# Attention of a hybrid encoder step: score products over all 128 partitions, value products in the array's two column halves, samples by zero-padded full-size products

## The chip, the cores and the metric

The kernel runs on one core of one Trainium2 chip. The metric is device time in microseconds, from the start of the program to its end. The kernel before took 2320.24 us (median of 3 runs, 2312.8 to 2323.56). TensorE (PE in the profile) multiplies; VectorE (DVE), ScalarE (ACT) and GpSimd (POOL) do the rest; SyncE (SP) issues the DMAs. Engines run beside each other, each one works through its own instructions in a fixed order, and semaphores hold an instruction back until what it reads is there or the buffer that it writes is free.

## The reference

One layer of an encoder, for 1024 tokens of a prompt and for 8 samples of 16 tokens each. From the normalised rows one projection makes the inputs of three mixers; their outputs are gated and summed, then follow an output projection, a norm, and a feed-forward block with a short convolution. Only the first mixer is touched here, attention over a sliding window: 8 query heads in two groups of 4, each group with one key head and one value head of 64 features, and one sink logit per head that takes part in the softmax but has no value.

```python
# prompt: every chunk of 64 tokens sees itself and the two chunks before it
s = jnp.einsum('bnqgrd,bnkgd->bngrqk', qc, kb, preferred_element_type=F32) * A_SCALE
s = jnp.where((key_pos >= 0)[None, :, None, None, None, :], s, NEG_BIG)
p = sink_softmax(s, sink[:, :, None, None])
o = jnp.einsum('bngrqk,bnkgd->bnqgrd', p.astype(v.dtype), vb)
# samples: 128 cached rows and the 16 new ones, no mask
kk = jnp.concatenate([k_cache.astype(k.dtype), k], axis=1)
s = jnp.einsum('bqgrd,bkgd->bgrqk', q, kk, preferred_element_type=F32) * A_SCALE
...
def sink_softmax(s, sink):
    m = jnp.maximum(s.max(-1, keepdims=True), sink)
    e = jnp.exp(s - m)
    return e / (e.sum(-1, keepdims=True) + jnp.exp(sink - m))
```

## The kernel before

The large products are a queue of blocks (`Queue`, `block`, L257 and L232): 128 columns of a weight by 384 tokens, 8 steps of depth 128, and three matmuls a step, since weights and inputs are held in two float32r parts each. These matmuls write a PSUM tile `psg`. After every second step `block` calls `tick`, which moves on generators that stand beside the queue (`beside`, L216): a generator yields the number of ticks until its next part. So the order in which the program is written mixes large products and small work; a scheduler then orders each engine's instructions by that and by what it holds ready, and may put large products ahead of a small one that waits. Attention (`attention`, L1414) is such a generator. It runs beside 21 blocks (`Q.run()`, L1419) and what is left of it follows in `drain`; then the PSUM banks are shared out anew (L1422), and the other two mixers begin. PSUM tiles here are `p1` (2 buffers), `ch` (2), `p2`, `ms`.

The prompt is worked through in 8 tiles of 128 tokens. `a_parts` splits queries and keys of a tile. Group 0 lies on partitions 0 to 63, group 1 on 64 to 127. `qs` holds a query's first part on the group's own half and its second part on the other half; `ks` holds the key's first part on both halves, `kl` the key's second part on the own half. `a_scores` makes a head's scores, 128 queries by 256 keys (128 in the first tile), with two matmuls into the same place: `qs` by `ks` over 128 partitions, and the own 64 partitions of `qs` by `kl`. DVE adds the mask and takes the maximum (L519, into `sm`, 3 buffers for two groups a tile). `a_out` takes the exponentials on ACT (L535, 8 a tile, with their sums), the sinks and the reciprocals; transposes the unnormalised probabilities on PE (16 a tile, 8 in the first; into `ch`, copied to `pT` by DVE and ACT in turn); multiplies `pT` as stationary operand by 64 columns of the values (2 x 8 matmuls a tile, float32, which PE makes in two passes); then multiplies by the reciprocals on DVE (L567), transposes the result with 4 more transposes, and stores it.

`a_samples` goes through the 8 samples one by one. The cached keys and values are loaded into `sm` buffers, the keys transposed to `kw`. Per sample there are four score products of 64 by 64 tiles of the array, an exponential over 144 keys, two transposes, four products with values (over 128 cached rows and over 16 new ones), a copy, one more transpose and a copy.

Of the kernel before, what the change touches and what calls it, by code (L numbers as in the profile page):

```python
# [45 lines left out]
def shape_constants():  # L46
# [17 lines left out]
    # s in the first half of a pair of blocks of b, t in its second half; columns for the second halves alone  # L64
# [7 lines left out]
def tile_encoder_step(ctx: ExitStack, tc: tile.TileContext, cst, x_prompt, x_sample, cache_k, cache_v, st_hgrn,  # L72
# [18 lines left out]
    # the banks of PSUM, shared out anew for each phase  # L91
# [77 lines left out]
    # per-feature vectors, features on partitions  # L169
# [29 lines left out]
    def prep(pieces, kt=KD, cols=P):  # L199
        """pieces: (part of the raw tile, DRAM view [p, k, c]); the exact two-part split of the weights"""  # L200
# [12 lines left out]
    # work that runs beside the large products: generators, moved on between their parts  # L213
# [18 lines left out]
    def block(hl, xh, xl, n, evict, kt=KD):  # L232
        """features on partitions: [128 columns of the weights, 384 tokens]"""
# [11 lines left out]
    def row_block(lh, ll, rhs, evict):  # L245
        """tokens on partitions: [128 tokens, 512 columns of the weights]"""
# [10 lines left out]
    class Queue:  # L257
        """Blocks of the large products in order; the weights of the next unit are made ahead."""
# [40 lines left out]
    def rsqrt(pool, x, n):  # L299
        """x ** -0.5 on [P, n]: an integer seed and three Newton steps"""  # L300
# [13 lines left out]
    def ln_group(pool, tiles, eps):  # L314
        """tiles: for each, its two halves of 512 features, tokens on partitions -> means and 1 / deviation"""
# [22 lines left out]
    def to_features(pool, xns, n, gname, bname, hi, lo):  # L338
        """normalised rows of three tiles -> scaled, features on partitions, in two parts"""
# [12 lines left out]
    # -mean / deviation and 1 / deviation of each input row: the residual is made anew from the input  # L352
# [51 lines left out]
    # ======== A: banded attention with sinks ========  # L404
# [28 lines left out]
    # the first two units: the tokens that are ready first  # L433
# [23 lines left out]
    # the norm weights carry the half of silu = x (1 + tanh(x/2)) / 2  # L457
# [27 lines left out]
    def a_parts(j):  # L485
        """queries: their two parts on the two halves of the partitions; keys: the first part on both halves, and
        the second; so a product of 128 rows and one of 64 make a score"""
# [3 lines left out]
        qs, ks, kl = small("qs", [P, 2, 4, P], 1, F32R), small("ks", [P, 2, 2 * P], 1, F32R), small("kl", [P, 2 * P], 1, F32R)  # L491
        for g, (a, b) in enumerate(((first, second), (second, first))):
# [3 lines left out]
            V.tensor_sub(kl[a, :w], k, ks[a, g, :w].bitcast(F32))  # L496
# [4 lines left out]
    def a_scores(j, parts):  # L501
# [6 lines left out]
        for g in range(2):  # L508
            gs = slice(64 * g, 64 * g + 64)
# [15 lines left out]
    def a_out(j, sc):  # L525
        kts, w, mx, sms = sc
# [13 lines left out]
        V.reciprocal(sums, sums)  # L540
        yield 2
        po = psum("ms")

        def products(g, i2, pT):
            for ii in range(2):
                i = 2 * i2 + ii
                for kt in range(nk):
                    mm(po[:, (2 * i + g) * 64:(2 * i + g + 1) * 64], pT[:, ii * nk + kt, :],
                       vT[:, kts[kt], 64 * g:64 * g + 64], start=(kt == 0), stop=(kt == nk - 1))

        last = None
        for g in range(2):
            for i2 in range(2):
                ps = psum("ch")
                for ii in range(2):
                    for kt in range(nk):
                        o = (ii * nk + kt) * P
                        tr(ps[:, o:o + P], sms[g][:, 2 * i2 + ii, kt * P:(kt + 1) * P])
                pT = small("pT", [P, 4, P], 2)
                (S.copy if i2 else V.tensor_copy)(pT[:, :2 * nk, :], u3(ps[:, :2 * nk * P]))  # L560
                if last is not None:
                    products(*last)
                last = (g, i2, pT)
                yield 1
        products(*last)
# [1274 lines left out]
```

## Time and profile before

| | us |
|---|---|
| median of 3 runs | 2320.24 |
| lowest, highest run | 2312.8, 2323.56 |
| span of the profiled execution, first to last instruction | 2315.3 |
| TensorE busy in that span | 2256.6 |
| attention beside large products, first score to the last large product | 120.5 to 297.9 |
| rest of attention, no large product beside it | 297.9 to 317.5 |

The profile shows one execution. Its span is told; a whole time for that execution, from start to end of the program, is not given apart from it, and the runs lie from 2.5 us under to 8.3 us over the span. The page gives busy time by engine and the chain of waits that ended last. Matmuls are pipelined: a matmul's length in the timeline holds the way through the array, and what one matmul costs in a row of matmuls is the distance from its start to the next one's start. A float32 product appears as two matmuls, one for each pass; float32r products as one.

### The profile page before, as it was taken

Reading aid. Unit: us, or ns where it says so; the run is one execution under the profiler, and the core shown is the slowest. Engines: PE = TensorE matmul, PEld = TensorE weight load, DVE = VectorE, ACT = ScalarE, POOL = GpSimd, SP = SyncE. Lnnn points to the kernel's source line nnn. Section 1 sums busy time; section 2 is a strip of 40 time slices with the busy share of each in tenths; the row PEclk is TensorE's granted clock in tenths of the full one; section 3 lists DMA queues with packets and bytes.
Section 4 is the critical chain, followed back from the end, with each engine's and each line's share of the span. In section 5 each row is a group of like instructions: output and inputs, shape, how many; then the busy total and the mean of one; then the engine's idle time right before and its main releaser. Section 6 shows DMA issues by size and latency. Waiting matters only on the chain.

```text
span 2315.3 us, 35344 instructions
## 1 busy us (share of the span) xinstructions
PE 2256.6 (97%) x13297; PEld 2101.9 (91%) x13297; DVE 1504.4 (65%) x4324; ACT 927.5 (40%) x2106; POOL 102.8 (4%) x74
## 2 busy tenths in 40 slices
PE   6999999999999999999999999999999999999996
PEld 6988989999999999999999978999999999999994
DVE  7256446667675657766777797676566566656669
ACT  4356434434344446354532333453334333432331
POOL 2000000000000000000000054000000000000004
PEclk9999989999999999999999999999999999999998
DMA  4111222222222221222354552321111110111112
GB/s 132 46 55 43 80 74 62 65 80 67 63 82 60 70 63 54 68 66 78 98 151 134 174 165 74 139 65 47 38 29 56 47 47 21 56 52 42 38 47 82
DMA packets 223836, 168.46 MB, mean 73 GB/s; under 512 B 34427, under 2 KB 213409, under 8 KB 223649
## 3 DMA queue, kind: packets, MB, share of 16 engines
q1 hardware_dynamic: 223664, 166.21, 24.0%
q8 instruction: 104, 1.70, 0.3%
q14 instruction: 68, 0.55, 0.1%
HBM read 126.91 MB, written 40.11 MB: 72 GB/s over the span
## 4 chain that ended last, share of the span: by engine, by line
PE 87%; DVE 7%; ACT 3%; DMA 2%; issue 1%; SPq 0%; POOL 0%; DVEq 0%; ACTq 0%
PE psg L107 72%; PE psp L107 6%; PE psch L107 4%; PE psp L147 2%; PE psms L107 2%; PE psch L147 1%; PE psms L147 1%; DVE yac L1787 1%; DVE lnst L321 1%; DMA x<-d_g 1%; ACT L1185 1%; ACT L1181 0%; DVE nwa L308 0%; DVE nwy L310 0%; DVE whl L206 0%
## 5 line engine op out<-in xcount | busy, mean ns | idle before, releaser
L107 PE MATMUL psg<-hh,whl 128*128 128x384 f32 x2976 | 812.6, 346 | 0.0
L107 PE MATMUL psg<-x1h,whl 128*128 128x384 f32 x2112 | 545.0, 336 | 1.2 <-ACT whl L205 1.2
L107 PEld LDWEIGHTS psg<-hh,whl 128*128 128x128 f32 x2976 | 537.7, 189 | 8.7 <-issue 3.6
L107 PE MATMUL psg<-hl,whl 128*128 128x384 f32 x1488 | 511.3, 344 | 1.5 <-POOL hl L347 1.3
L107 PEld LDWEIGHTS psg<-x1h,whl 128*128 128x128 f32 x2112 | 382.8, 188 | 3.2 <-ACT whl L205 1.5
L107 PE MATMUL psg<-x1l,whl 128*128 128x384 f32 x1056 | 355.5, 337 | 0.6 <-POOL x1l L347 0.6
L107 PEld LDWEIGHTS psg<-hl,whl 128*128 128x128 f32 x1488 | 281.5, 189 | 5.1 <-POOL hl L347 1.6
L107 PE MATMUL psg<-late,g 128*128 128x512 f32 x1080 | 251.2, 391 | 0.0
L107 PEld LDWEIGHTS psg<-late,g 128*128 128x128 f32 x1080 | 201.9, 188 | 42.9
L107 PEld LDWEIGHTS psg<-x1l,whl 128*128 128x128 f32 x1056 | 198.9, 188 | 1.7 <-POOL x1l L347 0.9
L206 DVE TENSOR_TENSOR whl<-wraw,whl 128x1024 fp32r<-128x1024 f32 (+1 forms) x122 | 144.2, 1183 | 68.0 <-ACT whl L205 66.9
L1758 DVE TENSOR_TENSOR yac<-yac,psg 128x512 f32<-128x512 f32 x180 | 123.5, 687 | 91.4 <-PE psg L107 88.0
L107 PE MATMUL psg<-o,whl 128*128 128x384 f32 x720 | 140.1, 345 | 3.1 <-DVE x L1464 1.7
L205 ACT CAST whl<-wraw 128x1024 fp32r<-128x1024 f32 (+1 forms) x122 | 121.4, 995 | 48.0 <-PE psg L107 24.7
L107 PEld LDWEIGHTS psg<-o,whl 128*128 128x128 f32 x720 | 125.8, 191 | 6.7 <-issue 2.1
L107 PE MATMUL psg<-wres,mixh 128*128 128x512 f32 x288 | 92.8, 395 | 3.6 <-DVE x L1464 2.7
L1718 DVE SCALAR_TENSOR_TENSOR va<-xp,fvec,va 128x384 f32<-128x384 f32 x132 | 82.0, 622 | 19.8 <-ACT va L1715 18.1
L1718 DVE SCALAR_TENSOR_TENSOR ga<-xp,fvec,ga 128x384 f32<-128x384 f32 x132 | 81.6, 620 | 8.2 <-ACT ga L1715 6.6
L1747 ACT CAST late<-wraw 128x1024 fp32r<-128x1024 f32 x20 | 20.1, 1047 | 162.6 <-PE psg L107 162.6
L1699 ACT COPY xp<-psg 128x384 f32<-128x384 f32 x88 | 42.2, 480 | 107.0 <-PE psg L107 106.8
L1399 ACT ACTIVATE ga<-psg 128x384 f32<-128x384 f32 x72 | 35.3, 491 | 104.0 <-PE psg L107 88.6
L1556 POOL TENSOR_TENSOR rows<-rows,gbin 128x1024 f32<-128x1024 f32 x9 | 27.7, 3078 | 1087.0 <-ACT rows L1555 1087.0
(449 smaller groups left out, 3260.1 us busy)
## 6 DMA issues: line engine op xcount, KB each, us to landing
wraw<-in_w_in_dram SPq DMA_DIRECT2D x58, 512.0 KB
wraw<-in_w_up_dram SPq DMA_DIRECT2D x44, 512.0 KB
d_g<-ga SPq DMA_DIRECT2D x72, 192.0 KB
wraw<-in_w_down_dram SPq DMA_DIRECT2D x22, 512.0 KB
acc<-d_g SPq DMA_DIRECT2D x48, 192.0 KB
d_o<-sq SPq DMA_DIRECT2D x24, 192.0 KB
xp<-d_o SPq DMA_DIRECT2D x24, 192.0 KB
x<-d_g SPq DMA_DIRECT2D x24, 192.0 KB
```

Source lines behind the costliest of these rows:

```text
L107: PE.matmul(out, lhsT, rhs, start=start, stop=stop)
L147: PE.transpose(out, in_, ident[:n, :n])
L205: S.copy(hl[:, 0, :kt, :cols], raw[:, :kt, :cols])
L206: V.tensor_sub(hl[:, 1, :kt, :cols], raw[:, :kt, :cols], hl[:, 0, :kt, :cols].bitcast(F32))
L321: V.bn_stats(out=st[:, i, :], in_=s_)
L1185: S.activation(s_, hd.f[n], AF.Exp, scale=-1.0)
L1399: S.activation(g, ps, AF.Tanh, scale=0.5)
L1556: G.tensor_mul(t, t, gb[:, 0])
L1699: S.copy(xp[:, 2:2 + NW], ps)
L1718: V.scalar_tensor_tensor(acc[:, :w], xp[:, j:j + w], fvec[:, j, ct:ct + 1], acc[:, :w], ALU.mult, ALU.add)
L1758: lambda ps: V.tensor_add(yac[j][:, cs], yac[j][:, cs], ps))
L1787: V.tensor_mul(y[:, sl], y[:, sl], gg)
```

## The change

Three parts, all in attention.

In `a_parts` the key's second part `kl` gets the shape of `ks`, [128, 2, 256], and is written to both halves (one subtraction more for each group). In `a_scores` the second matmul of a score then takes all 128 partitions of `qs` and `kl`, as the first does.

In `a_out` the probabilities are multiplied by the reciprocals before they are transposed, group 0 on DVE and group 1 on GpSimd. The loop over 128-key tiles is now outside: for each, the four heads of a group are transposed into one PSUM tile, and one product per group has 64 columns of the values as stationary operand, the four heads' probabilities as 512 moving columns, and its result on that group's 64 output partitions. The result is laid out as it is stored, so that the last four transposes and the multiplication on DVE go.

In `a_samples` the samples go two by two. A query tile `qz`, zero but for each group's own features and columns, makes all heads' scores of a sample in one product with `kw`, which now holds the new keys beside the cached ones. Probabilities stand in a zeroed tile `pn`, so that the 16 new rows can be multiplied with the values of all samples; products have the full 128 by 128 size.

```diff
@@ a_parts, a_scores
-        qs, ks, kl = small("qs", [P, 2, 4, P], 1, F32R), small("ks", [P, 2, 2 * P], 1, F32R), small("kl", [P, 2 * P], 1, F32R)
+        qs, ks, kl = small("qs", [P, 2, 4, P], 1, F32R), small("ks", [P, 2, 2 * P], 1, F32R), small("kl", [P, 2, 2 * P], 1, F32R)
...
-            V.tensor_sub(kl[a, :w], k, ks[a, g, :w].bitcast(F32))
+            for half in (a, b):
+                V.tensor_sub(kl[half, g, :w], k, ks[a, g, :w].bitcast(F32))
...
-                    mm(o, qs[gs, g, 2 * i2 + ii], kl[gs, :w], start=False, stop=True)
+                    mm(o, qs[:, g, 2 * i2 + ii], kl[:, g, :w], start=False, stop=True)
@@ a_out
+        for g in range(2):
+            sm = sms[g][:, :, :w]
+            (G if g else V).tensor_mul(sm, sm, bc(sums[:, 4 * g:4 * g + 4], 4, w))
         yield 2
         po = psum("ms")
 
-        def products(g, i2, pT):
...
-                    mm(po[:, (2 * i + g) * 64:(2 * i + g + 1) * 64], pT[:, ii * nk + kt, :],
-                       vT[:, kts[kt], 64 * g:64 * g + 64], start=(kt == 0), stop=(kt == nk - 1))
+        def products(kt, pTs):
+            for g in range(2):
+                mm(po[64 * g:64 * g + 64, :], vT[:, kts[kt], 64 * g:64 * g + 64], pTs[g],
+                   start=(kt == 0), stop=(kt == nk - 1))
...
-        for g in range(2):
-            for i2 in range(2):
+        for kt in range(nk):
+            pTs = []
+            for g in range(2):
                 ps = psum("ch")
...
+                for i in range(4):
+                    tr(ps[:, i * P:(i + 1) * P], sms[g][:, i, kt * P:(kt + 1) * P])
+                pTs.append(small("pT", [P, 4 * P], 3))
+                (S.copy if g else V.tensor_copy)(pTs[g], ps)
...
-        oa = small("oa", [P, 4, 2, 64])
-        V.tensor_mul(oa, po.rearrange("p (i g d) -> p i g d", i=4, g=2),
-                     sums.rearrange("p (g i o) -> p i g o", g=2, o=1).to_broadcast([P, 4, 2, 64]))
         yield 1
-        ps = psum("p2")
-        for i in range(4):
-            tr(ps[:, i * P:(i + 1) * P], oa[:, i].rearrange("p g d -> p (g d)"))
         of = small("oaf", [P, 4, P])
-        S.copy(of, u3(ps))
+        S.copy(of, u3(po))
@@ a_samples
+        kc, vw, qz = big(), big(), big()
...
+        G.memset(qz, 0.0)
+        for g in range(2):
+            gs = slice(64 * g, 64 * g + 64)
+            for i in range(4):
+                G.tensor_copy(qz[gs, :, 64 * g + TB * i:64 * g + TB * (i + 1)], bt(qf[i][gs, TPR:]))
+        kw = small("kw", [P, NB, KS])
+        G.tensor_copy(kw[:, :, P:], bt(kf[:, TPR:]))
...
+        def probabilities(r):
+            ps = psum("p1")[:, :2 * KS].rearrange("p (e k) -> p e k", e=2)
+            for e in range(2):
+                mm(ps[:, e], qz[:, 2 * r + e], kw[:, 2 * r + e])
...
+                V.tensor_scalar_mul(o[:, :P], pe[:, e, :P], sm2[:, e:e + 1])
+                V.tensor_scalar_mul(o[:, c:c + TB], pe[:, e, P:], sm2[:, e:e + 1])
...
+            for e in range(2):
+                for c in range(2):
+                    mm(po[:, e * P:(e + 1) * P], (vT[:, 8, :] if c else vw[:, 2 * r + e, :]),
+                       pT[:, (2 * e + c) * P:(2 * e + c + 1) * P], start=(c == 0), stop=(c == 1))
```

How the order changes is shown at three places. Names are those of the tiles, with a number for each use.

First, PE in the middle of the prompt's tiles. `psp` takes scores, `psms` products with values, `psch` transposed probabilities, `psg` large products. Before:

```order
L107 MATMUL psp_212_1471<-ks_1328,qs_1327 128x256
L107 MATMUL psp_212_1471<-kl_1329,qs_1327 128x256
L107 MATMUL psp_212_1471<-ks_1328,qs_1327 128x256
L107 MATMUL psp_212_1471<-kl_1329,qs_1327 128x256
L107 MATMUL psms_1524<-vT,pT_1530 128x64 x4
L147 MATMUL psch_1561<-call,sm_1312 128x128 x4
L107 MATMUL psms_1524<-vT,pT_1549 128x64 x4
L147 MATMUL psch_1578<-call,sm_1312 128x128 x4
L107 MATMUL psg_1747<-hl_2_129,whl_1217 128x384
```

After, products with values (`psms`) and the scores beside them:

```order
L107 MATMUL psp_268_1764<-ks_1609,qs_1608 128x256
L107 MATMUL psp_268_1764<-kl_1610,qs_1608 128x256
L107 MATMUL psp_268_1764<-ks_1609,qs_1608 128x256
L107 MATMUL psp_268_1764<-kl_1610,qs_1608 128x256
L107 MATMUL psms_1671<-pT_1703,vT 64x512
L107 MATMUL psms_1671<-pT_1731,vT 64x512
L107 MATMUL psg_2323<-hh_2_105,whl_1860 128x384
```

In place of four matmuls of 64 columns a head pair there stand two products of 512 columns next to each other, one for each group, and the score products have the same form throughout.

Second, PE where the large products beside attention run out. Before (`kw`, `kf` and `oa` are the samples' keys and queries, `obs` and `pTs` belong to the samples too):

```order
L107 MATMUL psg_3039<-hl_2_150,whl_2722 128x384
L107 MATMUL psg_3039<-hh_2_126,whl_2722 128x384
L107 MATMUL psp_517_3083<-kw_2673,oa_2689 64x128
L107 MATMUL psp_517_3083<-kf,oa_2689 64x16
L107 MATMUL psp_517_3083<-kw_2673,oa_2689 64x128
L107 MATMUL psp_517_3083<-kf,oa_2689 64x16
L147 MATMUL psp_459_2776<-call,obs_2755 128x64
L107 MATMUL psms_2841<-sm_2674,pTs_2819 64x64
L107 MATMUL psms_2841<-sm_2663,pTs_2819 64x64
L107 MATMUL psms_2841<-sm_2674,pTs_2819 64x64
L107 MATMUL psms_2841<-sm_2663,pTs_2819 64x64
```

After (`sm_2084` and `sm_2099` are the seventh tile's probabilities, `sm_2531` the cached keys, `sm_2250` the eighth tile's probabilities):

```order
L107 MATMUL psg_2911<-hl_2_150,whl_2630 128x384
L107 MATMUL psg_2911<-hh_2_126,whl_2630 128x384
L147 MATMUL psch_2357<-call,sm_2084 128x128 x4
L107 MATMUL psms_2330<-pT_2336,vT 64x512
L107 MATMUL psms_2330<-pT_2349,vT 64x512
L147 MATMUL psch_2389<-call,sm_2099 128x128 x4
L107 MATMUL psms_2330<-pT_2362,vT 64x512
L107 MATMUL psms_2330<-pT_2394,vT 64x512
L147 MATMUL psp_419_2547<-call,sm_2531 128x128 x4
L147 MATMUL psp_420_2553<-call,sm_2531 128x128 x4
L147 MATMUL psms_2476<-call,l_386_2377 27x128
L147 MATMUL psch_2455<-call,sm_2250 128x128 x4
```

Before, the last large product stands behind the score products of five samples, and the next one comes behind the last sample. After, it stands inside the seventh tile: the second half of that tile, the whole output of the eighth and all samples stand behind it without a large product between them, and the samples' cached keys are transposed ahead of the eighth tile's probabilities.

Third, ACT at the same place: `kw` takes the cached keys' transposes, rows with `pT` copy transposed probabilities. Before:

```order
L205 CAST whl_2722<-wraw_2720 128x1024
L574 COPY oaf_2534<-psp_412_2529 128x512
L603 COPY kw_2673<-psp_439_2677 128x512
L603 COPY kw_2673<-psp_440_2683 128x512
L560 COPY pT_2631<-psch_2626 128x512
L824 COPY xp_2763<-psg_2725 128x384
L838 ACTIVATE acc_2768<-xp_2763,vec 128x384
L842 ACTIVATE xp_2763<-acc_2768 128x384
```

After (rows with `sums` are the eighth tile's exponentials):

```order
L562 COPY pT_2394<-psch_2389 128x512
L843 COPY xp_2832<-psg_2799 128x256
L844 COPY xp_2832<-psg_2799 128x8x16
L571 COPY oaf_2416<-psms_2330 128x512
L606 COPY kw_2545<-psp_419_2547 128x4x128
L606 COPY kw_2545<-psp_420_2553 128x4x128
L537 ACTIVATE sm_2250,sums_2419<-sm_2250,anm_2421 128x256 x4
L537 ACTIVATE sm_2265,sums_2419<-sm_2265,anm_2421 128x256 x4
L540 ACTIVATE aes_2432<-aes_2432 128x8
```

The eighth tile's exponentials now stand behind the two copies of the samples' cached keys; before, all of the prompt's exponentials were ahead of these copies.

## Rows read from the trace of the kernel before

**Rows 1.** The page: span, engine PE, chain of waits by engine.
```profile
span 2315.3 us, 35344 instructions
...
PE 2256.6 (97%) x13297; PEld 2101.9 (91%) x13297; DVE 1504.4 (65%) x4324; ACT 927.5 (40%) x2106; POOL 102.8 (4%) x74
...
PE 87%; DVE 7%; ACT 3%; DMA 2%; issue 1%; SPq 0%; POOL 0%; DVEq 0%; ACTq 0%
```

**Rows 2.** Stretches of attention: busy us (instructions) by engine, granted clock, DMA share, GB/s.
```profile
120.50:297.90 177.40, 177.40 (x1087) 157.53 (x1087) 94.15 (x317) 92.81 (x265) 1.00 (x4) 0.99 0.20 59
297.90:317.50 19.60, 17.26 (x101) 10.94 (x101) 9.01 (x40) 8.63 (x35) 0.00 (x0) 0.61 0.13 40
317.50:322.80 5.30, 5.30 (x19) 5.20 (x19) 0.06 (x1) 1.32 (x7) 0.00 (x0) 0.50 0.42 118
```

**Rows 3.** Timeline of PE: start us, length us, line, op, out<-in, shapes, count.
```profile
148.40 0.33 PE L107 MATMUL psg<-hl,whl 128*128 128x384 f32 x1
148.58 0.34 PE L107 MATMUL psg<-hh,whl 128*128 128x384 f32 x1
148.75 1.00 PE L107 MATMUL psms<-vT,pT 128*128 128x64 f32 x8
149.56 0.36 PE L107 MATMUL psp<-ks,qs 128*128 128x256 f32 x1
149.85 0.38 PE L107 MATMUL psp<-kl,qs 64*128 64x256 f32 x1
150.17 0.38 PE L107 MATMUL psp<-ks,qs 128*128 128x256 f32 x1
```

**Rows 4.** PE groups by form, 120.5 to 317.5: count, busy us, mean ns, idle.
```profile
L107 PE MATMUL psp<-kl,qs 64*128 64x256 f32 x56 | 21.3, 381 | 0.0
L107 PE MATMUL psp<-ks,qs 128*128 128x256 f32 x56 | 20.1, 358 | 0.0
...
L107 PE MATMUL psms<-vT,pT 128*128 128x64 f32 x240 | 29.3, 271 | 0.0
...
L147 PE MATMUL psch<-call,sm 128*128 128x128 f32 x120 | 18.6, 285 | 0.0
...
L147 PE MATMUL psp<-call,oa 128*128 128x128 f32 x32 | 4.9, 276 | 0.0
```

**Rows 5.** Timeline of PE: a float32 product of 512 columns, two passes.
```profile
504.23 1.02 PE L107 MATMUL psch<-wx,kT 128*128 128x512 f32 x2
```

**Rows 6.** Timeline of PE around products that fill part of the array's columns.
```profile
893.02 0.26 PE L107 MATMUL psp<-mt 128*32 128x32 f32 x4
...
897.19 0.45 PE L107 MATMUL psp<-mt 128*64 128x64 f32 x4
897.57 0.49 PE L107 MATMUL psch<-r,u 128*128 128x128 f32 x2
```

**Rows 7.** Groups by form on ACT, DVE and POOL.
```profile
L535 ACT ACTIVATE sm<-sm,anm 128x256 f32<-128x256 f32 x56 | 27.7, 496 | 3.2 <-DVE anm L532 3.0
...
L519 DVE CUSTOM_DVE_ANT_0 sm<-psp,early 128x256 f32<-128x256 f32 x56 | 21.2, 421 | 16.9 <-PE psp L107 16.9
...
L206 DVE TENSOR_TENSOR whl<-wraw,whl 128x1024 fp32r<-128x1024 f32 x8 | 9.8, 1222 | 9.6 <-ACT whl L205 9.6
...
L603 ACT COPY kw<-psp 128x512 f32<-128x512 f32 x2 | 1.1, 591 | 1.4 <-PE psp L147 1.4
...
L606 POOL COPY oa<-qf 128x128 f32<-128x128 f32 x4 | 1.0, 296 | 223.2 <-PE psp L147 223.2
...
L1556 POOL TENSOR_TENSOR rows<-rows,gbin 128x1024 f32<-128x1024 f32 x9 | 27.7, 3078 | 1087.0 <-ACT rows L1555 1087.0
```

**Rows 8.** Timeline: the load of the samples' cached keys, and their transposes.
```profile
259.12 0.38 SPq L110 DMA_DIRECT2D sm<-in_cache_swa_k_dram  x1
...
264.21 0.27 PE L147 MATMUL psp<-call,sm 128*128 128x128 f32 x1
```

**Rows 9.** Timeline of POOL: the longest multiply of 128x1024.
```profile
1353.17 6.52 POOL L1556 TENSOR_TENSOR rows<-rows,gbin 128x1024 f32<-128x1024 f32 x1 [4.06 <-ACT rows L1555]
```

More of the change, by code (lines that the diff above doesn't have):

```diff
@@ L508, in a_scores @@
         for g in range(2):
-            gs = slice(64 * g, 64 * g + 64)
             sm = small("sm", [P, 4, 2 * P], 3)
@@ L590, in a_samples @@
     def a_samples():
-        vnew = small("sm", [P, 4, 2 * P], 3).rearrange("p a (b k) -> p (a b) k", b=2)[:TB]
-        for b in range(NB):
-            load(vnew[:, b, :], vT[16 * b:16 * b + 16, 8, :])
-        kc = small("sm", [P, 4, 2 * P], 3).rearrange("p a (b k) -> p (a b) k", b=2)
-        kw = small("kw", [P, NB, P])
-        vw = small("sm", [P, 4, 2 * P], 3).rearrange("p a (b k) -> p (a b) k", b=2)
+        KS = P + TB
+        big = lambda: small("sm", [P, 4, 2 * P], 3).rearrange("p a (b k) -> p (a b) k", b=2)
+        kc, vw, qz = big(), big(), big()
         load(kc, cache_k[0].rearrange("b t g d -> t b (g d)"))
         load(vw, cache_v[0].rearrange("b t g d -> t b (g d)"))
+        G.memset(qz, 0.0)
[5 more added lines that the diff above has]
+        G.tensor_copy(kw[:, :, P:], bt(kf[:, TPR:]))
         for i in range(2):
@@ L602, in a_samples @@
                 tr(ps[:, b * P:(b + 1) * P], kc[:, 4 * i + b, :])
-            S.copy(kw[:, 4 * i:4 * i + 4, :], u3(ps))
-        qg = small("oa", [P, NB, 4, TB])
-        for i in range(4):
-            G.tensor_copy(qg[:, :, i, :], bt(qf[i][:, TPR:]))
+            S.copy(kw[:, 4 * i:4 * i + 4, :P], u3(ps))
+        pn = small("sm", [P, 4, 2 * P], 3)
+        G.memset(pn, 0.0)
         oss = small("oaf", [P, 4, NB, TB])
-        for b in range(NB):
-            t0 = TPR + TB * b
-            ps = psum("p1")
+        def probabilities(r):
+            ps = psum("p1")[:, :2 * KS].rearrange("p (e k) -> p e k", e=2)
+            for e in range(2):
+                mm(ps[:, e], qz[:, 2 * r + e], kw[:, 2 * r + e])
+            mx = small("mxs", [P, 6], 3)
+            V.reduce_max(mx[:, 0:2], ps, axis=AX.X)
+            V.scalar_tensor_tensor(mx[:, 2:4], mx[:, 0:2], A_SCALE, sinkc.to_broadcast([P, 2]), ALU.mult, ALU.max)
+            V.tensor_scalar_mul(mx[:, 4:6], mx[:, 2:4], -1.0)
+            yield 1
+            pe = small("pes", [P, 2, KS], 1)
+            sm2 = small("sm2", [P, 4], 3)
+            for e in range(2):
+                S.activation(pe[:, e], ps[:, e], AF.Exp, bias=mx[:, 4 + e:5 + e], scale=A_SCALE, accum_out=sm2[:, e:e + 1])
+            V.tensor_sub(sm2[:, 2:4], sinkc.to_broadcast([P, 2]), mx[:, 2:4])
+            S.activation(sm2[:, 2:4], sm2[:, 2:4], AF.Exp)
+            V.tensor_add(sm2[:, 0:2], sm2[:, 0:2], sm2[:, 2:4])
+            V.reciprocal(sm2[:, 0:2], sm2[:, 0:2])
+            for e in range(2):
+                o, c = pn[:, 2 * (r % 2) + e], P + TB * (2 * r + e)
+                if r > 1:
+                    V.memset(o[:, c - 4 * TB:c - 3 * TB], 0.0)
+                V.tensor_scalar_mul(o[:, :P], pe[:, e, :P], sm2[:, e:e + 1])
+                V.tensor_scalar_mul(o[:, c:c + TB], pe[:, e, P:], sm2[:, e:e + 1])
@@ new lines, in a_samples @@
+        yield from probabilities(0)
+        for r in range(NB // 2):
+            if r + 1 < NB // 2:
+                yield from probabilities(r + 1)
+            yield 1
+            ps = psum("ch")
+            for e in range(2):
+                for c in range(2):
+                    tr(ps[:, (2 * e + c) * P:(2 * e + c + 1) * P], pn[:, 2 * (r % 2) + e, c * P:(c + 1) * P])
+            pT = small("pT", [P, 4 * P], 3)
+            S.copy(pT, ps)
+            yield 1
+            po = psum("ms")
+            for e in range(2):
+                for c in range(2):
+                    mm(po[:, e * P:(e + 1) * P], (vT[:, 8, :] if c else vw[:, 2 * r + e, :]),
+                       pT[:, (2 * e + c) * P:(2 * e + c + 1) * P], start=(c == 0), stop=(c == 1))
@@ L631, in a_samples @@
-            pT = small("pTs", [P, 2, P])
-            S.copy(pT[:, 0, :], ps2[:, :P])
-            S.copy(pT[:TB, 1, :], ps2[:TB, P:2 * P])
-            yield 1
-            ps3 = psum("ms")
-            for g in range(2):
-                gs = slice(64 * g, 64 * g + 64)
-                mm(ps3[:64, gs], pT[:, 0, gs], vw[:, b, gs], start=True, stop=False)
-                mm(ps3[:64, gs], pT[:TB, 1, gs], vnew[:, b, gs], start=False, stop=True)
-            ob = small("obs", [64, P])
-            V.tensor_copy(ob, ps3[:64, :P])
@@ L642, in a_samples @@
-            yield 1
-            ps4 = psum("p2")
-            tr(ps4[:, :64], ob)
-            S.copy(oss[:, :, b, :], bt(ps4[:, :64]))
+                (V.tensor_copy if g else S.copy)(
+                    oss[gs, :, 2 * r:2 * r + 2, :],
+                    po[gs, :2 * P].rearrange("p (e x) -> p e x", e=2)[:, :, 64 * g:64 * g + 64].rearrange(
+                        "p e (i t) -> p i e t", t=TB))
         store(d_o[0][:, TPR:].rearrange("(i p) t -> p i t", p=P), oss.rearrange("p i b q -> p i (b q)"))
```

30 lines of the change are left out of this document (2 added, 28 removed).

## Prediction

> **What bounds the kernel now.** The page comes first: TensorE is busy for 2256.6 of 2315.3 us, and the chain of waits is TensorE's for 87% [rows 1]. The table of stretches then says whether that holds where the change is made. From 120.5 to 297.9 us TensorE is busy for 177.40 of 177.40 us, VectorE for 94.15 and ScalarE for 92.81; from 297.9 to 317.5, with no large product left, TensorE has gaps and a granted clock of 0.61 [rows 2]. So in the first stretch the distance between starts of matmuls is what counts, and VectorE and ScalarE have some 47% to spare; in the second the chain between engines counts.
>
> The timeline gives the distances [rows 3]. A large matmul of 384 columns takes 0.174 us (148.40 to 148.58 to 148.75). The score products have only 256 columns, yet take 0.29 (149.56 to 149.85) and 0.32 (149.85 to 150.17): here a product in the 128*128 form follows one in the 64*128 form and the other way round. By columns alone 256 would be 0.174 x 256/384 = 0.12. Eight matmuls of the values take 0.81 (148.75 to 149.56), 0.10 each, though 64 columns would be 0.03. The mean lengths by form [rows 4] hold the way through the array and are not used as costs; their counts are.
>
> **The change part by part.** First stretch, before, by start distances: 492 large matmuls x 0.174 = 85.6; 112 wide scores x 0.30 and 16 of the first tile at about 0.25 = 37.6; 240 matmuls of the values x 0.10 = 24.2; 32 transposes of `oa` and 120 of the probabilities at 0.10, as for a matmul of few columns, = 3.2 and 12.0; 8 of the cached keys 0.8. That is 163.4; the other 14.0 of 177.4 are the samples' first part, small transposes and a stretch of lower clock.
>
> After, in the same stretch (until the large products run out):
> - Scores: 112 x 0.12 + 16 x 0.11 = 15.2. The price between is 0.12, if only the change of form cost time, and 0.30, if something else in these products does. I take 0.12, since the large matmuls, all of one form, run at 384/0.174 = 2.2 columns a ns, near one in each cycle of the 2.4 GHz level (granted clock 0.99, [rows 2]).
> - Values: 22 products of 512 columns, in 11 pairs. A float32 product of 512 columns takes 1.02 in two passes [rows 5], of which the way through the array is some 0.16 (0.33 less 0.174, [rows 3]); so 0.43 a pass. The two of a pair fill different column halves. If they run beside each other a pair costs 0.86, with 0.10 to come into the form, 0.10 to leave it and 0.05 for a second weight load: 1.11. If one after the other, 1.96. No row shows two 512-column products in different halves. The nearest are four products of 32 columns in four quarters, begun and ended within 0.26 us [rows 6], which leaves some 0.02 for each beyond the first's way; four one after another at 0.10 would be nearer 0.5. I take 1.11: 12.2.
> - Transposes: 96 of the probabilities x 0.10 = 9.6; those of `oa` are gone.
> - Large matmuls: 85.6 as before. Other: about 1.
>
> The sum is 123.6, which is 53.8 less. But not all of it is gained. Before, five samples' scores and all eight tiles were done when the last large matmul was issued; after, half of the seventh tile, the output of the eighth and all samples stand behind it, as the order of PE shows at its second place.
>
> Tail after, as a chain from the last large matmul:
> - The seventh tile's second half ends at about 2.4, which frees an `sm` buffer for the cached keys. Load to first transpose was 5.1 before (259.12 to 264.21, [rows 8]): 7.5. If the buffer were free earlier this falls away.
> - Eight transposes (0.8) and two copies on ScalarE of 0.59 [rows 7]: with waits 9.2.
> - ScalarE works in order, and its third place shows the eighth tile's eight exponentials behind those copies: 8 x 0.49 [rows 7] = 3.9, so 13.2; sinks and reciprocals 0.6, so 13.8.
> - The multiplication on GpSimd of 128 by 1024 took 3078 ns on average [rows 7] and up to 6.52 [rows 9], in a stage where VectorE and DMAs are at work; those of VectorE's size, 1222 [rows 7]. I take 3.1: 16.9.
> - 16 transposes, four copies and two pairs of products at the lower clock, some 5.2: 22.1.
> - The query tile `qz` needs a buffer, a memset (from 0.1 to 8 x 0.296 = 2.4) and eight copies at 0.296 or under [rows 7]; partly beside the above: 26.9.
> - The first two rounds of the samples, from scores to stored result, some 10 with every wait, and three more rounds at 2.8 each: 45.
>
> Before, that stretch was 19.6 [rows 2], in which the samples' 2.4 us rounds were already running. The 5.3 us at half clock that follow [rows 2] stay in both. So 177.4 + 19.6 = 197.0 becomes 123.6 + 45 = 168.6: 28.4 less. From this I take 1.5 for waits of TensorE in the first stretch: 27.
>
> What hides the rest: VectorE gains 16 subtractions of 0.42 (size as in L519) and 8 multiplications of 1.22 [rows 7], 16.5 us; with the 94.15 it stands at 111 of 124 us at most, before what it loses (the multiplication of `oa`, the samples). ScalarE loses nothing of size and stands at about 93 of 124. Within a tile, the way from a free `sm` buffer to the next is four masks and maxima (4 x 0.42), small steps 0.4, eight exponentials 3.9, sinks and reciprocals 0.7, a multiplication of 1.22 or 3.1: 8 to 10 us. TensorE has some 123.6/8 = 15 us of work a tile, of which about 12.5 lie between, so 2.7 to 4.5 us are spare. If that cover goes, every us over it counts about six times.
>
> After attention the orders differ by small swaps only, so no further term. The forecast is 27 less: on the profiled execution's own span 2315.3 - 27 = 2288, and from the median, which lies 4.9 over that span (the start and end of the program and the spread of the runs), 2320.2 - 27 = **2293 us**.
>
> **The rivals.**
> 1. The column halves run one after the other. Each pair then costs 1.96: 11 x 0.85 = 9.4 and four pairs in the tail 3.4 more, about 13 in all: 2306. For it: the products are long, and no row has two such. Against it: the quarters of [rows 6].
> 2. A middle way: the second half's first pass has to wait for the first half's second pass, since matmuls are issued in order and each product is two passes. A pair costs 0.43 more, 15 pairs 6: 2299. The Trainium skill, "TensorE: Matmul & The Clock Gate", section "The mechanism", says that matmuls start and end strictly in program order with no reordering; by that rule this rival would hold if a first pass shares time only with its neighbour. The rows here show only products too short to tell.
> 3. The tail keeps more than the 0.61 of the clock or its waits overlap better, so that it takes 35: 2283. For it: the chain above adds every wait in turn. Against it: TensorE idles in it even more than before.
> 4. Slower: the GpSimd multiplication decides in each tile. With 3.1 the way through a tile is 1.7 + 0.4 + 3.9 + 0.7 + 3.1 = 9.8 of the 12.5 between, so it is hidden up to 5.8 us; beyond that each of six tiles waits, and the tail takes the excess over 3.1 once. At the 6.52 of [rows 9] that is 6 x 0.7 + 3.4 = 7.6 of the gain: 2301. At 9.3 the gain of 27 is used up (6 x 3.5 + 6.2), and at 11 it is 6 x 5.2 + 7.9 = 39: 2332, slower than before. For it: one multiplication of this size took twice the mean, and beside VectorE's own work. Against it: the mean of nine is 3.08, and none reached 7. The Trainium skill, "GPSIMD Engine Reference", section "Specifications", says that this engine's path to SBUF is shared with VectorE, with contention where a VectorE instruction has two SBUF inputs. No row here takes the two apart; by this rule the long one of [rows 9] is what VectorE's subtractions and multiplications beside it make, which speaks for this rival.
> 5. The change does not do what it says: score products cost 0.30 in one form too. That takes 22 from the gain: 2315, and with the long tail it may be over 2320.
>
> **How the numbers follow.** The forecast has 0.66, with a range of its own of 2282 to 2304 (tail 35 to 50, waits up to 5). Rival 1 has 0.10, rival 2 0.06, rival 3 0.08, rival 4 0.06, of which 0.03 is slower than before by over 0.5%, rival 5 0.04, of which 0.01. The range of 2277 to 2311 takes in all but rival 5, the slow part of rival 4, and the ends of the others. About 0.5% (11.6 us) is what a measurement can tell from no change: faster lies under 2308.6, slower over 2331.8. Faster holds the forecast, rivals 2 and 3, most of 1 and half of 4: 0.87; same has rival 5 and the rest: 0.09; slower 0.04.
>
> **What would show it.** In the profile after: start distances of the score products at 0.12 (right) or near 0.3 (rival 5); two `psms<-pT,vT` products of a pair within about 1.1 (right), 1.5 (rival 2) or 1.9 (rival 1); the time from the last large matmul of attention to the next one at about 45 rather than 19.6, with a granted clock near 0.5; ScalarE's copies of `kw` ahead of the eighth tile's exponentials, with TensorE idle before their transposes; and TensorE's idle time before the `psch` transposes, put down to GpSimd's multiplication (rival 4). The forecast is wrong above all if the tail is much longer than 50 us, or if TensorE waits for more than 2 us in each tile.

## The result and the profile after

The changed kernel takes 2282.09 us (median of 4 runs, 2279.38 to 2285.45), the kernel before in the same comparison 2318.52 (2312.8 to 2323.56): ratio 0.9846, 95% interval 0.9829 to 0.9863. The forecast was 2293, with 2277 to 2311 as its range.

The page of the profiled execution, first the span, then TensorE and the other engines, then the chain of waits by engine, against [rows 1]:

```profile
span 2283.7 us, 34763 instructions
...
PE 2210.5 (97%) x12997; PEld 2061.2 (90%) x12997; DVE 1515.1 (66%) x4331; ACT 924.6 (40%) x2085; POOL 125.2 (5%) x89
...
PE 86%; DVE 7%; ACT 3%; DMA 2%; issue 1%; POOL 0%; SPq 0%; DVEq 0%; ACTq 0%; POOLq 0%
```

The span is 31.6 us shorter, and TensorE is busy for 46.1 less. So TensorE lost work, but a third of that came back as idle time. Where, the table of stretches tells (busy us and instructions of PE, PEld, DVE, ACT, POOL, then granted clock), from the first score to the last large product, from there to the next large product, and 5 us beyond; it answers to [rows 2]:

```profile
120.99:246.48 125.49, 125.49 (x766) 113.48 (x766) 89.94 (x272) 78.56 (x218) 18.09 (x7) 1.00 0.24 69
246.48:286.67 40.19, 23.93 (x117) 15.48 (x116) 21.24 (x86) 19.38 (x61) 6.74 (x11) 0.79 0.20 59
286.67:291.67 5.00, 5.00 (x30) 4.96 (x31) 2.53 (x9) 1.88 (x8) 0.00 (x0) 1.00 0.48 131
```

The first stretch shrank from 177 to 125.5, the second grew from 20 to 40.2, with TensorE idle for 16.3 of it. Together 165.7 in place of 197. (In the experiments both are counted from the first score to the next large product, by which the kernel before has 176.6 + 19.9 = 196.5.) TensorE's timeline around one group of scores and one pair of products of the values, against [rows 3]:

```profile
236.59 0.28 PE L107 MATMUL psp<-ks,qs 128*128 128x256 f32 x1
236.70 0.28 PE L107 MATMUL psp<-kl,qs 128*128 128x256 f32 x1
236.82 0.28 PE L107 MATMUL psp<-ks,qs 128*128 128x256 f32 x1
236.94 0.28 PE L107 MATMUL psp<-kl,qs 128*128 128x256 f32 x1
237.06 0.34 PE L107 MATMUL psg<-hh,whl 128*128 128x384 f32 x1
...
237.59 0.28 PE L107 MATMUL psp<-kl,qs 128*128 128x256 f32 x1
237.80 1.08 PE L107 MATMUL psms<-pT,vT 128*64 128x512 f32 x4
238.81 0.44 PE L107 MATMUL psg<-hl,whl 128*128 128x384 f32 x1
239.09 0.51 PE L107 MATMUL psg<-hh,whl 128*128 128x384 f32 x2
```

Scores now start 0.12 us apart (236.59, 236.70, 236.82, 236.94); before it was 0.30. The row with x4 is a pair of products, two passes each: 1.01 from its start to the next matmul's. The score ahead of it takes 0.21 instead of 0.12, and the large matmul behind it 0.28 (238.81 to 239.09) instead of 0.174, so with the changes of form a pair costs 1.20, where 1.11 was forecast. In the records the four matmuls start at 237.801, 237.807, 238.281 and 238.287: first pass of one half, first pass of the other, then the second passes.

In the second stretch TensorE's long waits are these (the bracket has the idle time before, and what ended it):

```profile
250.92 1.08 PE L107 MATMUL psms<-pT,vT 128*64 128x512 f32 x4 [1.37 <-DVE pT L562]
253.50 1.97 PE L147 MATMUL psp<-call,sm 128*128 128x128 f32 x8 [1.50 <-DMA sm<-in_cache_swa_k_dram]
255.26 0.42 PE L147 MATMUL psms<-call,l 128*27 128x128 f32 x1
262.15 1.09 PE L147 MATMUL psch<-call,sm 128*128 128x128 f32 x4 [6.47 <-DVE sm L545]
263.81 1.97 PE L147 MATMUL psch<-call,sm 128*128 128x128 f32 x8 [0.57 <-POOL sm L545]
...
269.57 1.25 PE L107 MATMUL psp<-kw,sm 128*128 128x144 f32 x8
```

The 6.47 us before the eighth tile's transposes are put down to VectorE's multiplication (L545), but that took 1.22; ScalarE's timeline shows what it stood behind:

```profile
255.51 0.58 ACT L606 COPY kw<-psp 128x512 f32<-128x512 f32 x1 [0.27 <-PE psp L147]
256.17 0.51 ACT L537 ACTIVATE sm<-sm,anm 128x256 f32<-128x256 f32 x1
...
259.63 0.49 ACT L537 ACTIVATE sm<-sm,anm 128x256 f32<-128x256 f32 x1
```

The eight exponentials begin right behind the copies of the cached keys, as the third piece of the order said. These copies are not alone in holding them: `anm`, which the exponentials read, was written only until 256.08. VectorE had it behind a copy that waited for TensorE's transpose at 255.26, and this one stood behind the transposes of the cached keys:

```profile
255.72 0.28 DVE L821 COPY r27c<-psms 27x128 f32<-27x128 f32 x1 [1.94 <-PE psms L147]
255.93 0.15 DVE L534 TENSOR_SCALAR anm<-am 128x8 f32<-128x8 f32 x1
```

### The profile page after: what moved, and what is told of

It is laid out like the page before. It is cut to its first block, busy times and chain, and to the rows that moved or that the text cites. A ratio compares the mean times of both kernels' runs of the same rounds, so it can differ in the third digit from the quotient of the medians.

```text
span 2283.7 us, 34763 instructions
## 1 busy us (share of the span) xinstructions
PE 2210.5 (97%) x12997; PEld 2061.2 (90%) x12997; DVE 1515.1 (66%) x4331; ACT 924.6 (40%) x2085; POOL 125.2 (5%) x89
## 4 chain that ended last, share of the span: by engine, by line
PE 86%; DVE 7%; ACT 3%; DMA 2%; issue 1%; POOL 0%; SPq 0%; DVEq 0%; ACTq 0%; POOLq 0%
PE psg L107 74%; PE psp L107 5%; PE psch L107 4%; PE psp L147 1%; PE psms L147 1%; PE psms L107 1%; PE psch L147 1%; DMA x<-d_g 1%; DVE yac L1799 1%; ACT L1197 1%; DVE lnst L321 0%; ACT L1193 0%; DVE mix L1477 0%; DMA wraw<-in_w_out_dram 0%; DVE mixl L1582 0%
## 5 line engine op out<-in xcount | busy, mean ns | idle before, releaser
L1730 DVE SCALAR_TENSOR_TENSOR va<-xp,fvec,va 128x384 f32<-128x384 f32 x132 | 82.0, 622 | 19.8 <-ACT va L1727 18.1
L1759 ACT CAST late<-wraw 128x1024 fp32r<-128x1024 f32 x20 | 20.1, 1047 | 162.6 <-PE psg L107 162.6
```

Of the source, the lines that this page charges most:

```text
L1730: V.scalar_tensor_tensor(acc[:, :w], xp[:, j:j + w], fvec[:, j, ct:ct + 1], acc[:, :w], ALU.mult, ALU.add)
L1759: S.copy(hl[:, 0], raw)
```

## Experiments

"First" is the stretch beside the large products, "second" from the last of them to the next one, both in us of the profiled execution; times are medians, ratios against the kernel before of the same comparison (its medians differ from one comparison to the next, as the first row shows, so that two kernels of different comparisons are compared by their ratios).

| kernel | first | second | both | time | ratio (95%) |
|---|---|---|---|---|---|
| before | 176.6 | 19.9 | 196.5 | 2314.7 to 2319.3 | 1 |
| changed | 125.5 | 40.2 | 165.7 | 2282.1 | 0.9846 (0.9829 to 0.9863) |
| 1 scores alone | 151.4 | 18.2 | 169.6 | 2294.2 | 0.9900 (0.9869 to 0.9932) |
| 2 values alone | 151.0 | 51.9 | 202.9 | 2325.8 | 1.0041 (1.0025 to 1.0058) |
| 3 samples alone | 176.9 | 6.6 | 183.5 | 2305.5 | 0.9952 (0.9933 to 0.9971) |
| 4 changed, old values | 152.6 | 4.1 | 156.7 | 2279.3 | 0.9844 (0.9816 to 0.9872) |
| 5 one column half | 140.3 | 33.8 | 174.1 | 2291.1 | 0.9894 (0.9863 to 0.9924) |
| 6 all on VectorE | 125.8 | 41.1 | 166.9 | 2283.9 | 0.9853 (0.9833 to 0.9872) |
| 7 four buffers | 140.7 | 16.2 | 157.0 | 2274.4 | 0.9811 (0.9789 to 0.9834) |
| 8 both of 6 and 7 | 137.8 | 18.2 | 156.0 | 2273.4 | 0.9808 (0.9780 to 0.9836) |
| 9 more buffers | 142.0 | 13.2 | 155.3 | 2276.5 | 0.9813 (0.9792 to 0.9835) |
| 10 pairs kept | 136.2 | 12.6 | 148.8 | 2263.4 | 0.9763 (0.9745 to 0.9781) |

**1 to 3: each part alone.** Number 1 has the hunks of `a_parts` and `a_scores`, 2 those of `a_out`, 3 those of `a_samples`, each on the kernel before.

Scores, expected: 

> The kernel before with the change of the scores alone (both products of a score on 128 partitions; the samples' saved key rows stand in another buffer so that the tiles fit). Theory: the alternation of forms was the cost, so 112 score products fall from 0.30 to 0.12 us and 16 from 0.25 to 0.11, 22 us less in the stretch beside the large products (177 to 155), and the part behind it stays near 20: about 2297. Rival: the second part of the key costs time for another reason (its place, its split), the pitch stays near 0.3: 2318.

Values, expected: 

> The kernel before with the change of the values alone (probabilities normalised first, products of 512 columns in column halves; the old samples' queries stand in another buffer so that the tiles fit). Theory: TensorE saves 17.6 us (24.2 + 3.2 + 12.0 of matmuls and transposes become 12.2 + 9.6), but a tile's way gets longer by the multiplication, so the large products run out before the samples begin, as after the whole change; the part behind them grows from 20 to 45 or 50 us: 2315, little or nothing gained. Rival: what TensorE saves is gained: 2301.

Samples, expected: 

> The kernel before with the change of the samples alone. Theory: the four rounds of two samples are short enough to stand beside the large products; the part without large products falls from 20 to about 4, the stretch beside them stays near 177: 2301. Rival: the samples are as late as before and the part behind stays at 15 or more: 2314.

The stretches of 1, of 2 and of 3, in this order (columns as in the result, then DMA share and GB/s):

```profile
120.98:272.39 151.41, 151.41 (x1081) 148.16 (x1081) 99.00 (x334) 92.73 (x268) 1.00 (x4) 1.00 0.24 69
272.39:290.55 18.16, 16.70 (x102) 10.66 (x101) 8.61 (x37) 7.75 (x32) 0.00 (x0) 0.68 0.14 43
```

```profile
121.07:272.05 150.98, 150.98 (x767) 120.76 (x766) 85.09 (x260) 79.17 (x218) 17.25 (x7) 1.00 0.19 58
272.05:323.93 51.88, 38.07 (x206) 22.85 (x205) 23.20 (x98) 22.31 (x81) 3.84 (x5) 0.63 0.16 47
```

```profile
120.91:297.81 176.90, 176.90 (x1076) 159.03 (x1076) 96.47 (x340) 96.32 (x277) 4.92 (x10) 0.99 0.20 58
297.81:304.43 6.62, 3.37 (x19) 2.59 (x18) 2.77 (x7) 2.21 (x5) 0.00 (x0) 0.79 0.38 109
```

In 1 and 3 the theory holds: the scores give 26.9 of attention's 196.5, the samples 13.0 (20.6 and 9.2 in the medians). In 2 it holds in kind, and misses in size: the values alone save 25.6 beside the large products (151.0 for 176.6, part of it samples that moved out) and add 32.0 behind them, and the kernel is 0.4% slower than before, where no loss was expected.

**4: the changed kernel without the part on the values.**

> The changed kernel with the old products of the values (scores and samples changed, the values not). If the change of the values carries its 17.6 us of TensorE into the time, this is slower than the changed kernel by that: 2299. Theory: that saving is given back by the longer way of a tile; without it the samples stand beside the large products, attention takes 155 beside them and about 3 behind: 2278, as fast as the changed kernel or up to 8 us faster.

```profile
120.93:273.56 152.63, 152.63 (x1085) 151.13 (x1085) 102.62 (x357) 96.50 (x278) 3.80 (x10) 1.00 0.23 68
273.56:277.65 4.09, 1.52 (x11) 1.13 (x10) 1.84 (x4) 1.58 (x3) 0.00 (x0) 1.00 0.13 48
```

In the profiled executions attention is 9.0 us shorter without the values' part than with it (156.7 and 165.7), and 39.8 shorter than before, which is what 1 and 3 give together (26.9 + 13.0). The times don't show the 9 us: the ratios are 0.9844 and 0.9846. So the whole gain of the change is that of scores and samples, and the values' part gains nothing here; that it costs something in the whole change is seen in the profiles alone (by itself, in number 2, it costs 0.4% of the time). The values' part shortens the first stretch by 27.1 us and lengthens the second by 36.1.

**5: both groups in one column half.**

```diff
-                mm(po[64 * g:64 * g + 64, :], vT[...], pTs[g], ...)
+                mm((pq if g else po)[:64, :], vT[...], pTs[g], ...)
```

> The changed kernel with the products of both groups on the same 64 output partitions, that is in the same column half of the array, in two PSUM tiles; the copy of the result takes two instructions of half the partitions. Theory: the halves work beside each other only if they are different; a pair of products (four matmuls, 1.01 us from its start to the next matmul's in the changed kernel) takes about 1.9, 11 pairs beside the large products make that stretch 9 us longer (135), the part behind it 2 to 3: 2293. Rival: the passes follow each other anyway and the pair is short for another reason: still 1.0, 2282.

```profile
239.08 1.07 PE L107 MATMUL psms<-pT,vT 128*64 128x512 f32 x2
239.99 1.02 PE L107 MATMUL psp<-pT,vT 128*64 128x512 f32 x2
240.94 0.66 PE L147 MATMUL psch<-call,sm 128*128 128x128 f32 x4
```

Same sizes, same form, next to each other, only the same half: 0.91 + 0.95 = 1.86 for the pair instead of 1.01. (Of the 12 pairs beside the large products 7 are parted by other work in this kernel; they take 2 x 1.00.) The theory of the halves holds. Attention is 8.4 longer, and not 12, and by other terms than expected: the first stretch is 14.8 longer, the second 6.4 shorter, since more of the work now lies beside large products and of the second stretch's idle time 8.8 us are left (33.75 less 24.93 busy) in place of 16.3:

```profile
261.24:294.99 33.75, 24.93 (x106) 15.67 (x105) 16.40 (x61) 16.76 (x54) 6.74 (x11) 0.80 0.22 61
```

**6: GpSimd's multiplication on VectorE.**

```diff
-            (G if g else V).tensor_mul(sm, sm, bc(...))
+            V.tensor_mul(sm, sm, bc(...))
```

> The changed kernel with both groups' probabilities multiplied on VectorE. In the changed kernel GpSimd's 2.84 us end 2.98 after VectorE's multiplication begins, and VectorE's subtractions beside it take 1.25 instead of 0.42. Theory: the two engines keep each other out of the same tile memory; two multiplications on VectorE take 2.44 in a row, and no subtraction is stretched, so each tile's way is 0.5 to 1.5 shorter and attention 4 to 8 us (165.7 to about 160): 2277. Rival: GpSimd's multiplication is hidden, and VectorE gets 8 x 1.22 = 9.8 us more to do: 2282 to 2288.

The theory rested on these rows of the changed kernel, VectorE's and then GpSimd's:

```profile
206.66 1.22 DVE L545 TENSOR_TENSOR sm<-sm,sums 128x1024 f32<-128x1024 f32 x1
207.85 2.50 DVE L497 TENSOR_TENSOR kl<-kf,ks 64x256 fp32r<-64x256 f32 x2
...
211.39 0.85 DVE L497 TENSOR_TENSOR kl<-kf,ks 64x256 fp32r<-64x256 f32 x2
```

```profile
206.80 2.84 POOL L545 TENSOR_TENSOR sm<-sm,sums 128x1024 f32<-128x1024 f32 x1 [19.13 <-DVE sums L542]
224.86 2.84 POOL L545 TENSOR_TENSOR sm<-sm,sums 128x1024 f32<-128x1024 f32 x1 [15.22 <-ACT oaf L571]
239.77 2.84 POOL L545 TENSOR_TENSOR sm<-sm,sums 128x1024 f32<-128x1024 f32 x1 [12.07 <-ACT oaf L571]
```

Two subtractions take 2.50 while GpSimd multiplies (until 209.64) and 0.85 when it doesn't. One by one, only the first is long, 2.07, and ends 0.28 behind GpSimd's multiplication; the second takes its 0.42, so that the 1.25 of the expectation is a mean of two unlike ones. The Trainium skill, "GPSIMD Engine Reference", section "Specifications", has this engine's SBUF interface shared with VectorE, with contention for VectorE instructions with two SBUF inputs; the trace agrees. At one place in number 7 (below) GpSimd's multiplication began first, and there it took 1.89, and VectorE's instruction beside it 2.90 where the same form takes 1.22 [rows 7]:

```profile
176.99 1.89 POOL L545 TENSOR_TENSOR sm<-sm,sums 128x1024 f32<-128x1024 f32 x1 [8.71 <-DVE sums L542]
```

```profile
177.07 2.90 DVE L206 TENSOR_TENSOR whl<-wraw,whl 128x1024 fp32r<-128x1024 f32 x1 [0.25 <-ACT whl L205]
```

So by these rows some 0.95 of the 2.84 (2.84 less 1.89) comes with VectorE's multiplication, which began 0.14 before it. This contention costs nothing all the same: with all of it on VectorE, attention takes 166.9, 1.2 more. My theory that it lengthens attention falls, the rival holds.

**7 and 8: a fourth buffer for probabilities.** GpSimd's rows above also show how slow a tile is: the multiplications start 18 and 15 us apart there, and 15 to 22 over all full tiles, more than the 12.5 of TensorE's work that I had put between. Three buffers for two groups a tile let only one group of the next tile begin before this one is transposed. In the kernel with four, the samples' output stands in a buffer of `qs`:

```diff
-            sm = small("sm", [P, 4, 2 * P], 3)
+            sm = small("sm", [P, 4, 2 * P], 4)
...
-                pTs.append(small("pT", [P, 4 * P], 3))
+                pTs.append(small("pT", [P, 4 * P], 2))
...
-        of = small("oaf", [P, 4, P])
+        of = small("pT", [P, 4 * P], 2).rearrange("p (i t) -> p i t", i=4)
```

> The changed kernel with four buffers for probabilities instead of three; to fit, transposed probabilities have two buffers instead of three and share them with the tile that is stored. Theory: the tile's way is long because the second group of the next tile waits for a buffer; with four the next tile's scores and maxima are done before, the eighth tile is out before the large products end, and only the samples stand behind them: 131 beside and 26 behind, 157 in place of 165.7: 2274. Rival: what limits a tile is the order exponentials, multiplication, transposes, copies itself, or the fewer buffers behind: no gain, 2282 or more.

> Both: four buffers for probabilities, and both multiplications on VectorE. Theory: the gains add, 153 for attention: 2270. Rival, if VectorE or the buffers limit: 2278 or more.

```profile
120.93:261.67 140.74, 140.74 (x815) 118.96 (x815) 103.46 (x309) 87.64 (x247) 22.76 (x18) 1.00 0.24 71
261.67:277.88 16.21, 11.75 (x68) 7.33 (x67) 10.42 (x48) 9.48 (x33) 0.00 (x0) 1.00 0.22 63
```

Number 7 is as the theory has it in sum (157.0 for 157), but that is luck: the second stretch is 16, not 26, and the first 10 longer than expected. The tiles do come faster: from the second tile's first exponential to the seventh's it is 15.5 us a tile, against 18.2 in the changed kernel. It is 13.0 in number 4, which has three buffers too, so that three buffers are slow only together with the values' longer way. Number 8 cannot be told from 7, as number 6 alone gained nothing either. The first stretch should have been near 131, and the order of PE shows why it wasn't. With the copies to `pT` at other times, 8 of 15 pairs of products had other work between their two products; 7 of them lie in the first stretch, and its products take 20.1 us there in place of the 13.1 that 13 whole pairs would.

**9 and 10: pairs parted and pairs kept.** Number 9 has three buffers for `pT` again (two small tiles from ahead of attention share buffers of others to make room) and results of products in two PSUM banks in turn. Number 10 is 9 and this, which pins group 0's product behind group 1's:

```diff
-            for g in range(2):
-                mm(po[64 * g:64 * g + 64, :], ...)
+            for g in (1, 0):
+                ins = PE.matmul(po[64 * g:64 * g + 64, :], ...)
+            tc.keep_in_program_order(ins)
```

> The changed kernel with four buffers for probabilities, three for transposed ones (also used for the tile that is stored), and the results of products taken in turn in two PSUM banks. In the order of PE 6 of the 15 pairs of products have other instructions between their two products (8 of 15 with four buffers before this, none in the changed kernel). Theory: a pair that is parted costs 1.9 in place of 1.0, since each half works alone; so the stretch beside the large products is about 5 longer than with whole pairs: 138, and the part behind, with the samples in two banks, 12 in place of 16: 150 for attention, 2268. Rival: parted pairs cost nothing since large products stand between them: 145.

> The same, and the pairs held together: group 1's product is issued first and group 0's pinned behind it (14 of 15 pairs next to each other). Theory: 5 pairs x 0.9 = 4.5 us less than with parted pairs: 145 to 146 for attention, 2263, the fastest of all. Rival: holding a product back delays others, and the time is as with parted pairs: 2268.

TensorE in number 9, a parted product and a whole pair:

```profile
226.26 1.07 PE L107 MATMUL psp<-pT,vT 128*64 128x512 f32 x2
227.26 0.45 PE L107 MATMUL psg<-hh,whl 128*128 128x384 f32 x1
...
239.47 1.08 PE L107 MATMUL psms<-pT,vT 128*64 128x512 f32 x4
240.48 0.66 PE L147 MATMUL psch<-call,sm 128*128 128x128 f32 x4
```

One product alone takes 1.00 of TensorE's time (226.26 to 227.26), two as neighbours 1.01 (239.47 to 240.48). Number 9 is a miss (2276 for 2268, and 155.3 of attention for 150: it gained nothing on 7). Number 10 is the fastest of all, 6.5 us shorter in attention than 9, of which the five pairs that are no longer parted make 5:

```profile
120.89:257.12 136.23, 135.95 (x823) 118.67 (x823) 104.40 (x311) 89.09 (x254) 22.55 (x18) 1.00 0.25 76
257.12:269.70 12.58, 8.55 (x60) 6.97 (x60) 8.77 (x45) 7.70 (x25) 0.00 (x0) 1.00 0.20 58
```

That its median is the 2263 expected is partly luck: attention took 148.8 and not 145 to 146, and of the 14.5 us between the spans of the profiled executions of 9 and 10 (2276.1 and 2261.6) 8 lie behind attention, between some 1000 and 1460 us, where both do the same work. With the eighth tile's output beside large products, only the samples' last rounds are left behind them, and the values' part is worth something now: 148.8 against the 156.7 of number 4, with ratios of 0.9763 and 0.9844 whose intervals don't overlap. Number 4 was not run with four buffers; with TensorE busy for all of its first stretch, and only 4.1 us in the second, there is little for them to gain, but that is argued and not shown.

## Why the prediction was right, and where it was not

**The size.** 27 us were forecast, and 2293 us. Attention gave 31 (197 to 165.7), the spans differ by 31.6, and the medians by 36.4. The 4.8 between spans and medians are the spread of executions: the changed kernel's profiled one took 2285.45, 3.4 over its median and 1.75 over its span; if that 1.75 holds for the kernel before as well, its profiled one took 2317.1, 1.5 under its median. The 4.9 that I set between span and median was thus mostly spread. So of the 9 us that the medians gave beyond the forecast about half are attention's, and the rest lies in that spread.

**First stretch.** 123.6 and 1.5 of waits were forecast, 125.5 measured. By start distances the scores take 15.5 (15.2 forecast), the 22 products 11.1 (12.2), the transposes 10.0 (9.6), the large matmuls 88.3 (85.6), and other small work 0.6 (1). Some of the changes of form that I had put to the products are in the large matmuls. They took 91.3 before, so that 5.7 of the 14.0 that I gave to other work were theirs. The 0.05 for a second weight load inside a pair is shown by no run: the second product starts 0.006 behind the first.

**Second stretch.** 45 forecast, 40.2 measured. The chain was the right one and nearly each step came within 1 us: after the last large product the cached keys' transposes begin at 7.0 (7.5), their copies end at 9.6 (9.2), the exponentials at 13.6 (13.2), GpSimd's multiplication at 17.3 (16.9), the eighth tile's products at about 23 (22.1). The mis-sized term is `qz`: I added 4.8 for its memset and copies, but they run from 265.90 on beside the eighth tile's last transposes and products, and the first scores of the samples start at 23.1, without a wait for them. From there to the end it is 17.1, where I had 18.1; but I counted five rounds of two samples, and there are four, so that a round takes longer than I had it. The buffer for the cached keys came free at 3.1 and not 2.4, and the load took 3.9 and not 5.1.

**What failed.** First, "if that cover goes, every us over it counts": I counted on waits of TensorE in each tile, with 2.7 us or more to spare. TensorE has no such wait: in the first stretch it is idle for 0.3 us at most in all of these kernels; what a late tile does is to let large products run ahead, and the bill comes when they run out. With 15 to 22 us from tile to tile the spare time was below nothing, and number 7 shows that the three buffers have a part in it (15.5 us a tile with four, 18.2 with three). Second, I did not ask what each part is worth by itself. The sum was right, but the values' part in it gained nothing: attention is 9 us longer with it by the profiles, and the times are the same (number 4). Third, the half clock behind attention did not stay: the granted clock is 1.00 from 286.67 on, where it was 0.50 before. TensorE runs 30 matmuls there in 5.00 us, where the kernel before ran 19 in 5.30 [rows 2]; by these rows I estimate a gain of some 2 us that I had left out. Of the parts alone, number 1, with the old samples, has 0.50 still in the 5 us behind, number 3, with the new ones, 0.59, and number 4, with both, 1.00; why is open.

**The rivals.** The first, halves one after the other, falls: 1.01 and not 1.96; only in one and the same half is it 1.86 (number 5). The second, the middle way, falls too: the two products do start in order, as the Trainium skill has it ("TensorE: Matmul & The Clock Gate", section "The mechanism"), but in these records the passes of neighbours alternate, so each pass has its partner beside it. The kernel before could have told this: the four rows at 893.02 [rows 6] are not four products in four quarters, as I read them, but two products with two passes each, in two quarters (the kernel writes partitions 0 to 31 and 64 to 95 there), and they start at 893.025, 893.032, 893.077 and 893.084, which is the same alternation. The third, a tail of 35, came half true: it took 40.2, between 35 and 45, with a granted clock of 0.79 and with `qz` beside other work; that the time is within 1 us of this rival's 2283 is owed to the spread as well. The fourth: GpSimd's multiplication took 2.84 in each of the seven full tiles, and does not decide (number 6). The fifth, scores at 0.30 in one form: they start 0.12 apart in the changed kernel, and number 1 shows the gain by itself.

## What to carry to other kernels

An engine that shows no idle time may only be eating its cover early: compare the pace of the small work (start to start of one step in each tile) with the large work that is there to cover it, and see what stands behind the last of it. Part a change and price each part by the end of that stretch, not by the engine time it saves. Where two half-width products are to share the array, the instruction order tells whether they are still neighbours; a buffer more or less elsewhere can part them.

## What the hardware showed

- Two float32 products of 512 columns in different column halves cost 1.01 us as neighbours, one alone 1.00, two in the same half 1.86.
- A matmul in the form of its neighbour starts by its columns (256 in 0.12, 384 in 0.174); a change between 128*128 and 64*128 made the same product 0.30.
- Beside GpSimd's multiplication, a subtraction of VectorE took 2.07 in place of 0.42 and ended 0.28 behind it. GpSimd's multiplication took 2.84 where VectorE's began 0.14 before it, and 1.89 where it began with VectorE idle (twice in number 7). Beside one of these, even a copy of 3 columns on VectorE, begun 0.03 behind it, took 1.89 in place of 0.16 (at 228.54).
